# Row-wise argmax over 8192 x 8192 floats: loads and maxima cut into column pieces, index arithmetic gathered into one step

## The chip, the core and the metric

The kernel runs on one core of a Trainium2 chip. The metric is the device time of one execution in microseconds (us). Before the change the median of three runs is 655.53 us (655.39 to 655.56); every run was at a granted clock of 1.0. Times are compared with runs of the kernel before on the same chip, in the same rounds. A ratio is the mean time of one kernel's runs over that of the other's of the same rounds, so it is not quite the ratio of the medians that stand beside it.

Engines in the profile: DVE is VectorE, POOL is GpSimd, ACT is ScalarE, PE is TensorE, SP is SyncE, and SPq is the queue on which SyncE issues loads.

## The reference

```python
def setup_inputs():
    return {"x": np.random.randn(8192, 8192).astype(np.float32)}

def reference(x):
    return np.argmax(x, axis=1)
```

The input has 268 MB and is read once. The output is 8192 integers.

## The kernel before

The rows are worked in 64 tiles of 128 rows; a tile is 128 partitions by 8192 columns, 4 MiB. For each tile, VectorE takes the maximum of each of 128 chunks of 64 columns. For every four tiles a lookup follows: the maximum over the chunks (`mx`), which chunk has it (`match` on GpSimd, then `k` on VectorE), a gather of that chunk from HBM, and the place in it (`match` again, then `k2`). Lookups are put off by some steps, so that VectorE need not wait for GpSimd or the gather. Tiles 62 and 63, the last two, go another way: right after its maxima VectorE finds the largest chunk of such a tile itself (`MAX8` and `FIND_INDEX8` in the timelines), so the second `MAX8` of a timeline marks the end of the last maximum.

```python
xpool = ctx.enter_context(tc.tile_pool(name="x_sbuf", bufs=5))
...
def load_reduce(t, cm, widths):
    xt = xpool.tile([P, M], F32, tag="xt")
    at = 0
    for w in widths:
        keep(nc.sync.dma_start(out=xt[:, at:at + w], in_=x[t * P:(t + 1) * P, at:at + w]))
        at += w
    at = 0
    for w in widths:
        c0, c1 = at // L, (at + w) // L
        keep(nc.vector.reduce_max(
            out=cm[:, c0:c1], in_=xt[:, at:at + w].rearrange("p (c l) -> p c l", l=L), axis=AX.X))
        at += w
        step[0] = t * 4 + at // 2048
        run_due()
...
def finish():                       # the end of a group's lookup
    k2 = spool.tile([P, g], F32, tag="k2")
    keep(nc.vector.reduce_max(out=k2, in_=wl, axis=AX.X))
    r = res[:, t0:t0 + g]
    keep(nc.vector.scalar_tensor_tensor(out=r, in0=k, scalar=float(L), in1=k2, op0=ALU.mult, op1=ALU.add))
    keep(nc.vector.tensor_scalar(out=r, in0=r, scalar1=-1.0, scalar2=float(C * L + L), op0=ALU.mult, op1=ALU.add))
    if t0 + g == 60:
        store(0, 60)
...
for g in [4] * 15 + [2]:
    ...
        load_reduce(t, cm[:, i, :], [M] if t < 60 else [2048] * 4)
    ...
load_reduce(62, cm62, [2048] * 4)
d62 = direct_begin(62, cm62)
load_reduce(63, cm63, [2048] * 3 + [1024, 512, 512])
d63 = direct_begin(63, cm63)
```

Tiles 60 to 63 are already loaded in quarters and smaller pieces; the others come whole, one DMA each.

Of the kernel before, what the change touches and what calls it, by code (L numbers as in the profile page):

```python
# [7 lines left out]
F32 = mybir.dt.float32  # L8
U32 = mybir.dt.uint32
I32 = mybir.dt.int32  # L10
ALU = mybir.AluOpType
AX = mybir.AxisListType
# [3 lines left out]
def kernel(  # L16
# [5 lines left out]
    nc = tc.nc  # L22
    keep = tc.keep_in_program_order
    N, M = x.shape
    P = 128
    C = 128
    L = M // C
    NT = N // P

    xpool = ctx.enter_context(tc.tile_pool(name="x_sbuf", bufs=5))  # L30
    spool = ctx.enter_context(tc.tile_pool(name="small", bufs=3))
    cpool = ctx.enter_context(tc.tile_pool(name="const", bufs=1))
# [30 lines left out]
    keep(nc.gpsimd.tensor_scalar(out=ident, in0=ident, scalar1=0.0, scalar2=None, op0=ALU.is_equal))  # L63

    res = cpool.tile([P, NT], F32)
    o_last = cpool.tile([P, 2], I32)
    nc.gpsimd.memset(o_last, 0)

# [4 lines left out]
    def defer(steps, fn):  # L73
        pending.append((step[0] + steps, fn))
        pending.sort(key=lambda e: e[0])

    def run_due():
        while pending and pending[0][0] <= step[0]:
            pending.pop(0)[1]()

    def load_reduce(t, cm, widths):

        assert sum(widths) == M
# [14 lines that stand above are left out]
    def match(w, vals, mx, desc, g):  # L98

        for i in range(g):  # L100
            keep(nc.gpsimd.tensor_scalar(out=w[:, i, :], in0=vals[:, i, :], scalar1=mx[:, i:i + 1],  # L101
                                         scalar2=None, op0=ALU.is_equal))
            keep(nc.gpsimd.tensor_tensor(out=w[:, i, :], in0=w[:, i, :], in1=desc, op=ALU.mult))  # L103

    def store(t0, n):
        ps = ppool.tile([n, P], F32, tag="ps")
        nc.tensor.transpose(ps, res[:, t0:t0 + n], ident)  # L107
        o = cpool.tile([n, P, 2], I32, tag=f"o{t0}")
        nc.gpsimd.memset(o, 0)  # L109
        keep(nc.scalar.copy(out=o[:, :, 0:1], in_=ps.unsqueeze(2)))  # L110
        keep(nc.scalar.dma_start(out=out_rows[t0:t0 + n, :], in_=o.rearrange("t p two -> t (p two)")))

    def lookup(t0, g, cm, gather_after, match_after):

        mx = spool.tile([P, g], F32, tag="mx")
        keep(nc.vector.reduce_max(out=mx, in_=cm, axis=AX.X))  # L116
        wc = spool.tile([P, g, C], F32, tag="wc")
        match(wc, cm, mx, descC, g)
        k = spool.tile([P, g], F32, tag="k")

        def gather():
            keep(nc.vector.reduce_max(out=k, in_=wc, axis=AX.X))  # L122
            idx = spool.tile([P, g], U32, tag="idx")
            keep(nc.vector.tensor_tensor(out=idx, in0=baseC[:, t0:t0 + g], in1=k, op=ALU.subtract))  # L124
            ga = spool.tile([P, g, L], F32, tag="ga")
            for i in range(g):
                keep(nc.gpsimd.indirect_dma_start(  # L127
                    out=ga[:, i, :], out_offset=None, in_=x_flat[:, :],
                    in_offset=bass.IndirectOffsetOnAxis(ap=idx[:, i:i + 1], axis=0)))
            wl = spool.tile([P, g, L], F32, tag="wl")  # L130
            match(wl, ga, mx, descL, g)

            def finish():
                k2 = spool.tile([P, g], F32, tag="k2")
                keep(nc.vector.reduce_max(out=k2, in_=wl, axis=AX.X))  # L135

                r = res[:, t0:t0 + g]
                keep(nc.vector.scalar_tensor_tensor(out=r, in0=k, scalar=float(L), in1=k2,  # L138
                                                    op0=ALU.mult, op1=ALU.add))
                keep(nc.vector.tensor_scalar(out=r, in0=r, scalar1=-1.0, scalar2=float(C * L + L),  # L140
                                             op0=ALU.mult, op1=ALU.add))
                if t0 + g == 60:
                    store(0, 60)

            defer(match_after, finish)

        defer(gather_after, gather)

    def direct_begin(t, cm):

        m8 = spool.tile([P, 8], F32, tag="m8")
        keep(nc.vector.max(out=m8, in_=cm))  # L152
        c8 = spool.tile([P, 8], U32, tag="c8")
        keep(nc.vector.max_index(out=c8, in_max=m8, in_values=cm))  # L154
        idx = spool.tile([P, 1], U32, tag="idx1")
        keep(nc.vector.tensor_tensor(out=idx, in0=c8[:, 0:1], in1=base[:, t:t + 1], op=ALU.add))  # L156
        ga = spool.tile([P, L], F32, tag="ga1")
        keep(nc.gpsimd.indirect_dma_start(  # L158
            out=ga, out_offset=None, in_=x_flat[:, :],
            in_offset=bass.IndirectOffsetOnAxis(ap=idx[:, :1], axis=0)))  # L160
        return m8, c8, ga

    def direct_end(m8, c8, ga, dst):
        l8 = spool.tile([P, 8], U32, tag="l8")
        keep(nc.vector.max_index(out=l8, in_max=m8, in_values=ga))  # L165
        keep(nc.vector.scalar_tensor_tensor(out=dst, in0=c8[:, 0:1], scalar=float(L), in1=l8[:, 0:1],
                                            op0=ALU.mult, op1=ALU.add))

    t = 0
    for g in [4] * 15 + [2]:  # L170
        cm = spool.tile([P, g, C], F32, tag="cm")
        t0 = t
        for i in range(g):
            load_reduce(t, cm[:, i, :], [M] if t < 60 else [2048] * 4)
            t += 1
        if g == 4:
            lookup(t0, g, cm, 4, 7)
        else:
            lookup(t0, g, cm, 1, 100)

    cm62 = spool.tile([P, C], F32, tag="cm1")
    load_reduce(62, cm62, [2048] * 4)
    d62 = direct_begin(62, cm62)
    cm63 = spool.tile([P, C], F32, tag="cm1")
    load_reduce(63, cm63, [2048] * 3 + [1024, 512, 512])
    d63 = direct_begin(63, cm63)
    step[0] = 1000
    run_due()
    direct_end(*d62, res[:, 62:63])
    store(60, 3)  # L190
    direct_end(*d63, o_last[:, 0:1])
# [31 lines left out]
```

## Time and profile before

| | before |
|---|---|
| time, median | 655.53 us |
| span of the profiled run | 653.8 us |
| VectorE busy | 592.0 us (91%) |
| share of the 16 DMA engines taken by the loads of x | 96.3% |
| a whole tile: spacing of landings, without gathers | 9.71 us |
| a whole tile: its maximum on VectorE | 8.69 us |
| last piece of x lands | 636.7 us |
| VectorE ends the last maximum | 645.2 us |

The prediction below shows the lines that these come from. The chain of work that ended last, by engine (share of the span):

```profile
DMA 77%; DVE 19%; issue 2%; POOL 1%; SPq 0%; POOLq 0%; DVEq 0%
```

### The profile page before, as it was taken

What the parts mean: (1) busy time and instruction counts of PE and PEld (TensorE: products, weight loads), DVE (VectorE), ACT (ScalarE), POOL (GpSimd) and SP (SyncE); (2) the same over time, 40 slices, a digit from 0 to 9 for tenths busy, and PEclk for the clock granted to TensorE, in tenths of its full rate; (3) what the DMA queues carried; (4) which work ended last, traced back from release to release, by engine and by line L of the source; (5) the groups of instructions that cost most, each with busy time, mean ns of one, the idle gap of its engine ahead of it and who ended that gap; (6) DMA issues with size and microseconds to landing.
All of it is one profiled execution on the core that took longest, in us unless ns stands there. A gap on an engine that the chain in (4) does not pass through costs nothing.

```text
span 653.8 us, 739 instructions
## 1 busy us (share of the span) xinstructions
PE 0.8 (0%) x2; PEld 0.2 (0%) x2; DVE 592.0 (91%) x188; ACT 1.8 (0%) x3; POOL 176.0 (27%) x325
## 2 busy tenths in 40 slices
PE   0000000000000000000000000000000000000000
PEld 0000000000000000000000000000000000000000
DVE  2899898998989989998998989989998998989986
ACT  0000000000000000000000000000000000000000
POOL 1004223041241313323041240412323142230550
DMA  9999999999999999999999999999999999999980
GB/s 385 419 447 419 425 447 424 419 433 429 429 425 431 429 429 423 423 443 425 421 439 423 426 425 435 433 424 429 423 437 425 421 443 421 427 425 415 418 341 4
DMA packets 13511, 270.66 MB, mean 414 GB/s; under 512 B 2434, under 2 KB 2497, under 8 KB 3905
## 3 DMA queue, kind: packets, MB, share of 16 engines
q1 hardware_dynamic: 11376, 268.44, 96.3%
q0 software_dynamic: 2048, 2.10, 0.9%
q10 hardware_dynamic: 81, 0.06, 0.0%
q14 instruction: 6, 0.05, 0.0%
HBM read 270.53 MB, written 0.07 MB: 414 GB/s over the span
## 4 chain that ended last, share of the span: by engine, by line
DMA 77%; DVE 19%; issue 2%; POOL 1%; SPq 0%; POOLq 0%; DVEq 0%
DMA xt<-in_x_dram 76%; DVE cm L92 18%; DMA ga<-in_x_dram,idx 1%; POOL ga L127 0%; SPq L87 0%; POOL wc L101 0%; POOL ga L158 0%; DVE k L122 0%; POOL wc L103 0%; DVE mx L116 0%; POOL wl L101 0%; DVE k L135 0%; DVE c L154 0%; DVE idx L124 0%; POOL wl L103 0%
## 5 line engine op out<-in xcount | busy, mean ns | idle before, releaser
L92 DVE TENSOR_REDUCE cm<-xt 128x128 f32<-128x8192 f32 (+2 forms) x78 | 556.9, 7152 | 51.5 <-DMA xt<-in_x_dram 51.5
L101 POOL TENSOR_SCALAR wc<-cm,mx 128x128 f32<-128x128 f32 x62 | 37.2, 601 | 256.3 <-DVE mx L116 256.3
L127 POOL DMA_INDIRECT ga<-in_x_dram,idx x62 | 60.3, 972 | 96.9 <-DVE idx L124 82.9
L101 POOL TENSOR_SCALAR wl<-ga,mx 128x64 f32<-128x64 f32 x62 | 27.6, 445 | 98.2 <-DMA ga<-in_x_dram,idx 98.2
L103 POOL TENSOR_TENSOR wc<-wc,descC 128x128 f32<-128x128 f32 x62 | 28.1, 453 | 5.2
L103 POOL TENSOR_TENSOR wl<-wl,descL 128x64 f32<-128x64 f32 x62 | 19.7, 319 | 5.2
L122 DVE TENSOR_REDUCE k<-wc 128x4 f32<-128x512 f32 (+1 forms) x16 | 10.6, 660 | 1.7 <-POOL wc L103 1.7
L116 DVE TENSOR_REDUCE mx<-cm 128x4 f32<-128x512 f32 (+1 forms) x16 | 10.7, 669 | 0.6
L135 DVE TENSOR_REDUCE k<-wl 128x4 f32<-128x256 f32 (+1 forms) x16 | 6.4, 400 | 0.0
L158 POOL DMA_INDIRECT ga<-in_x_dram,idx x2 | 2.0, 994 | 9.1 <-DVE k L135 8.8
L140 DVE TENSOR_SCALAR res<-res 128x4 f32<-128x4 f32 (+1 forms) x16 | 2.7, 170 | 0.6
L138 DVE SCALAR_TENSOR_TENSOR res<-k,k 128x4 f32<-128x4 f32 (+1 forms) x16 | 2.7, 167 | 0.6
L124 DVE TENSOR_TENSOR idx<-baseC,k 128x4 uint32<-128x4 f32 (+1 forms) x16 | 2.6, 162 | 0.6
L110 ACT CAST o<-ps 60x128 int32<-60x128 f32 (+1 forms) x2 | 0.5, 263 | 645.4 <-PE ps L107 645.4
L165 DVE MATCH_VALUE_LOAD l<-m,ga 128x8 f32 x2 | 0.2, 88 | 1.6 <-DMA ga<-in_x_dram,idx 1.6
L107 PE MATMUL ps<-ident,res 128*60 128x128 f32 (+1 forms) x2 | 0.8, 382 | 646.9 <-DVE res L140 633.3
L110 ACT ACT_TABLE_LOAD x1 | 1.3, 1283 | 0.7 <-PEq L207 0.7
L152 DVE MAX8 m<-cm 128x8 f32<-128x128 f32 x2 | 0.6, 295 | 0.1
L109 POOL MEMSET o<- 60x256 int32 (+1 forms) x2 | 0.6, 302 | 0.0
L154 DVE FIND_INDEX8 c<-m,cm 128x8 uint32<-128x128 f32 x2 | 0.6, 284 | 0.0
L63 POOL TENSOR_SCALAR ident<-ident 128x128 f32<-128x128 f32 x1 | 0.5, 539 | 0.0
L156 DVE TENSOR_TENSOR idx<-c,base 128x1 uint32<-128x1 uint32 x2 | 0.4, 206 | 0.1
(15 smaller groups left out, 2.6 us busy)
## 6 DMA issues: line engine op xcount, KB each, us to landing
xt<-in_x_dram SPq DMA_DIRECT2D x60, 4096.0 KB, 40.6
xt<-in_x_dram SPq DMA_DIRECT2D x15, 1024.0 KB, 21.3
ga<-in_x_dram,idx POOLq DMA_INDIRECT x64, 8.3
xt<-in_x_dram SPq DMA_DIRECT2D x1, 512.0 KB, 17.9
xt<-in_x_dram SPq DMA_DIRECT2D x2, 256.0 KB, 13.8
out_dram<-o ACTq DMA_DIRECT2D x1, 60.0 KB, 2.9
out_dram<-o ACTq DMA_DIRECT2D x1, 3.0 KB
out_dram<-o_last SPq DMA_DIRECT2D x1, 1.0 KB, 3.1
```

Source lines behind the costliest of these rows:

```text
L92: keep(nc.vector.reduce_max(out=cm[:, c0:c1], in_=xt[:, at:at + w].rearrange("p (c l) -> p c l", l=L), axis=AX.X))
L101: keep(nc.gpsimd.tensor_scalar(out=w[:, i, :], in0=vals[:, i, :], scalar1=mx[:, i:i + 1], scalar2=None, op0=ALU.is_equal))
L103: keep(nc.gpsimd.tensor_tensor(out=w[:, i, :], in0=w[:, i, :], in1=desc, op=ALU.mult))
L110: keep(nc.scalar.copy(out=o[:, :, 0:1], in_=ps.unsqueeze(2)))
L116: keep(nc.vector.reduce_max(out=mx, in_=cm, axis=AX.X))
L122: keep(nc.vector.reduce_max(out=k, in_=wc, axis=AX.X))
L124: keep(nc.vector.tensor_tensor(out=idx, in0=baseC[:, t0:t0 + g], in1=k, op=ALU.subtract))
L127: keep(nc.gpsimd.indirect_dma_start(out=ga[:, i, :], out_offset=None, in_=x_flat[:, :], in_offset=bass.IndirectOffsetOnAxis(ap=idx[:, i:i ...
L135: keep(nc.vector.reduce_max(out=k2, in_=wl, axis=AX.X))
L138: keep(nc.vector.scalar_tensor_tensor(out=r, in0=k, scalar=float(L), in1=k2, op0=ALU.mult, op1=ALU.add))
L140: keep(nc.vector.tensor_scalar(out=r, in0=r, scalar1=-1.0, scalar2=float(C * L + L), op0=ALU.mult, op1=ALU.add))
L158: keep(nc.gpsimd.indirect_dma_start(out=ga, out_offset=None, in_=x_flat[:, :], in_offset=bass.IndirectOffsetOnAxis(ap=idx[:, :1], axis=0)))
```

## The change

Its intent is to let VectorE begin on a tile before all of it has landed, to release work sooner, and to save VectorE two small operations for each group of four tiles. Tiles 0 to 47 come in halves, 48 to 61 in quarters, 62 and 63 in quarters and smaller pieces. The index of 60 tiles is computed by two operations on 60 columns instead of by two for each group.

```diff
+    k_all = cpool.tile([P, NT], F32)
+    k2_all = cpool.tile([P, NT], F32)
 ...
+    def combine(t0, n):
+        r = res[:, t0:t0 + n]
+        keep(nc.vector.scalar_tensor_tensor(out=r, in0=k_all[:, t0:t0 + n], scalar=float(L),
+                                            in1=k2_all[:, t0:t0 + n], op0=ALU.mult, op1=ALU.add))
+        keep(nc.vector.tensor_scalar(out=r, in0=r, scalar1=-1.0, scalar2=float(C * L + L),
+                                     op0=ALU.mult, op1=ALU.add))
 ...
             def finish():
-                k2 = spool.tile([P, g], F32, tag="k2")
-                keep(nc.vector.reduce_max(out=k2, in_=wl, axis=AX.X))
-                (two operations for r, as in the kernel before)
+                keep(nc.vector.reduce_max(out=k2_all[:, t0:t0 + g], in_=wl, axis=AX.X))
                 if t0 + g == 60:
+                    combine(0, 60)
                     store(0, 60)
 ...
-            load_reduce(t, cm[:, i, :], [M] if t < 60 else [2048] * 4)
+            load_reduce(t, cm[:, i, :], [4096] * 2 if t < 48 else [2048] * 4)
 ...
-    load_reduce(62, cm62, [2048] * 4)
+    load_reduce(62, cm62, [2048] * 3 + [1024] * 2)
 ...
-    load_reduce(63, cm63, [2048] * 3 + [1024, 512, 512])
+    load_reduce(63, cm63, [2048] * 2 + [1024] * 3 + [512] * 2)
 ...
+    combine(60, 2)
```

More of the change, by code (lines that the diff above doesn't have):

```diff
@@ L118, in lookup @@
         match(wc, cm, mx, descC, g)
-        k = spool.tile([P, g], F32, tag="k")
+        k = k_all[:, t0:t0 + g]
         def gather():
@@ L133, in finish @@
             def finish():
-                k2 = spool.tile([P, g], F32, tag="k2")
-                keep(nc.vector.reduce_max(out=k2, in_=wl, axis=AX.X))
-                r = res[:, t0:t0 + g]
-                keep(nc.vector.scalar_tensor_tensor(out=r, in0=k, scalar=float(L), in1=k2,
-                                                    op0=ALU.mult, op1=ALU.add))
-                keep(nc.vector.tensor_scalar(out=r, in0=r, scalar1=-1.0, scalar2=float(C * L + L),
-                                             op0=ALU.mult, op1=ALU.add))
+                keep(nc.vector.reduce_max(out=k2_all[:, t0:t0 + g], in_=wl, axis=AX.X))
                 if t0 + g == 60:
+                    combine(0, 60)
                     store(0, 60)
```

## The prediction

> **What bounds the kernel now.** I read the page first, then the timeline of VectorE at the start and the end, then the SyncE queue's timeline and windows over the last 60 us.
>
> ```profile
> span 653.8 us, 739 instructions
> PE 0.8 (0%) x2; PEld 0.2 (0%) x2; DVE 592.0 (91%) x188; ACT 1.8 (0%) x3; POOL 176.0 (27%) x325
> ...
> DMA  9999999999999999999999999999999999999980
> ...
> q1 hardware_dynamic: 11376, 268.44, 96.3%
> ```
>
> The 16 DMA engines are full from the first slice to the 38th, while VectorE has idle time in every tile. The queue of x alone takes 96.3% of the span. So the load stream sets the pace, and VectorE follows it. The chain of waits agrees: 76% of the span is "DMA xt", 18% is the maximum of line 92. That share of line 92 is no proof that VectorE bounds: the chain runs through it where a buffer is given back, and the queue is four tiles ahead then. VectorE at the start shows the tile time of the stream without any lookup beside it:
>
> ```profile
> 12.91 8.69 DVE L92 TENSOR_REDUCE cm<-xt 128x128 f32<-128x8192 f32 x1 [12.91 <-DMA xt<-in_x_dram]
> 22.61 8.69 DVE L92 TENSOR_REDUCE cm<-xt 128x128 f32<-128x8192 f32 x1 [1.02 <-DMA xt<-in_x_dram]
> ...
> 51.75 8.69 DVE L92 TENSOR_REDUCE cm<-xt 128x128 f32<-128x8192 f32 x1 [0.30 <-DMA xt<-in_x_dram]
> ```
>
> Each starts when its tile has landed: (51.75 - 12.91) / 4 = 9.71 us a tile, against 8.69 us for its maximum. Later a group of four tiles takes 39.45 us (a reduce waiting for its tile starts at 506.58 and the fourth after it at 546.04), so the group's four gathers cost the stream about 0.6 us.
>
> The end is another matter, and the change is aimed at it. Windows over the end (columns: length, busy time and instructions of each engine, clock, DMA share, GB/s) and VectorE's timeline there:
>
> ```profile
> 633.00:636.00 3.00, 0.39 (x1) 0.13 (x1) 2.93 (x5) 0.27 (x1) 1.23 (x4) 1.00 0.64 227
> 636.00:639.00 3.00, 0.00 (x0) 0.00 (x0) 2.96 (x4) 0.00 (x0) 1.35 (x2) 1.00 0.07 17
> 639.00:645.00 6.00, 0.00 (x0) 0.00 (x0) 6.00 (x5) 0.00 (x0) 0.00 (x0) 1.00 0.00 0
> ```
>
> ```profile
> 636.24 8.97 DVE L92 TENSOR_REDUCE cm<-xt 128x32 f32<-128x2048 f32 x6
> 645.25 0.29 DVE L152 MAX8 m<-cm 128x8 f32<-128x128 f32 x1
> ```
>
> The DMA engines fall silent at about 636 us; the last piece, issued at 624.1, lands 12.6 us later, at 636.7. VectorE has all six pieces of the last tile still before it and ends them at 645.2: 8.5 us after the data. The lag comes from tile 59, the last one taken whole: it lands at 595.3, when VectorE can only begin its 8.69 us. The quarters of tiles 60 to 63 then land faster than it can catch up. From 645.2 to the end (8.6 us) are the last lookup, its gather and the store, which the change leaves alone.
>
> **What the Trainium skill says.** "Perfetto Trace Analysis", section DMA Optimizations: splitting may let work start sooner if DMA engines are generally idle, and larger transfers use the bandwidth better. Here they are not idle (digit 9 in 38 slices), so only the last, uncovered wait can gain. "DMA: Bandwidth & Descriptors", section Why small descriptors are slow: each packet bears a fixed overhead besides its bytes; it gives 3 cycles on 256 B and says the combining of descriptors is worth it only up to 256 B. One would call it nothing at 16 KB. The trace shows more at 8 KB. The pieces of tiles 60 on are issued when an earlier piece has landed (the queue's own waits name landings for 69 issues), so their spacing is the spacing of landings:
>
> ```profile
> 595.33 15.23 SPq L87 DMA_DIRECT2D xt<-in_x_dram  x7
> ```
>
> The seventh issue starts 0.33 us (one issue) before the end of this piece, at 610.23: (610.23 - 595.33) / 6 = 2.483 us for 1 MB, before any gather of this stretch. Four make 9.93 us against 9.71 whole. So three more DMAs cost 0.22 us, **0.074 us for each DMA added** (8 more row packets and one completion write on each of 16 engines). The windows agree: 421 GB/s in 598 to 614, 434 in 13 to 51.7. "Vector Engine (DVE) Microarchitecture Reference", section Measured stream behaviour on trn2: 1.0417 ns a column plus about 75 ns an instruction after overlap. The trace: 8686 ns for 8192 columns, 2276 for 2048, 1204 for 1024, 672 for 512, which is 1.043 ns a column plus 139 ns; back to back they overlap by 81 ns (8.97 us for pieces that sum to 9.38), which leaves 58 (so 2.195 us for a quarter behind another, 1.12 for 1024 columns, 0.59 for 512).
>
> **The change part by part.**
> - *Smaller pieces, the stream.* Tiles 0 to 47 have one more DMA each (48), tiles 48 to 59 three more (36), tiles 62 and 63 one each (2): 86 x 0.074 = **6.4 us later at the end of the stream**, all of it on the path. Of this the halves are 3.6 us, taken by a straight line between two measured sizes. The last landing moves from 636.7 to 643.1.
> - *Smaller pieces, VectorE before the end.* A half should take 1.043 x 4096 + 139 = 4.41 us, two of them 8.82. Even with 0.5 us a tile for lookups that stays under the stream's 9.8, so it costs nothing. The same holds for quarters (8.86 against 9.93).
> - *Smaller pieces, the end.* VectorE now works on pieces as they land and has no 8.69 us lag. I count back from 643.1 with 2.48 us for a 2048-column piece, 1.28 for 1024, 0.68 for 512 (the slope 2.41 us per MB plus 0.074): tile 63 has two, three and two of them, tile 62 three and two, so tile 62's first piece lands at 643.1 - 17.7 = 625.4. Is VectorE free then? Tile 59 lands at 595.3 + 6.2 = 601.5; its last quarter 2.28, tile 60 8.86, tile 61 8.86, and between them two row maxima and a gather step (0.6, 0.8, 0.4) make 21.8: it is done at 623.3 and waits. From 625.4 its work has no room left: tile 62 in 3 x 2.195 + 2 x 1.12 + 0.08 = 8.9; column maximum and index 0.53 (627.39 to 627.92 before); the finish of tiles 56 to 59 with the index step 0.71 (632.31 to 633.02); the direct start of tile 62 0.90; tile 63 in 2 x 2.195 + 3 x 1.12 + 2 x 0.59 = 8.9. Sum 19.95, end **645.4**. The data bound would be 643.1 + 0.7 = 643.8, so VectorE binds the end still, by 1.6 us. The 1.66 us wait for GpSimd before that column maximum should go: GpSimd was done at 627.4, VectorE asks at about 627.7.
> - *Index arithmetic in one step.* 14 of 15 groups lose two small operations, 0.71 - 0.41 = 0.30 us each with gaps, 4.2 us of VectorE. All of it lies in idle time (51.5 us waited for tiles), so it is worth nothing. The one step on 60 columns costs some hundredths more and stays in the end.
> - *Start.* VectorE starts at about 8 instead of 12.9 us; it has only to wait sooner. Worth nothing.
>
> Sum: the last maximum ends at 645.4 instead of 645.2. A gain of 6.2 us of lag is spent on 6.4 us of stream. Time 655.5 + 0.2, rounded for the small extra waits between the pieces in the end to **656.0 us**.
>
> **The rivals.**
> - *Extra DMAs are free.* The stream would end at 636.7 again and VectorE 6.4 us sooner: 649.4 us, 0.9% faster. For it: packets of one engine overlap a little (DMA shares of 1.01 in windows), and the skill's overhead is tiny. Against it: six spacings of 2.483 and 421 GB/s. Between the two lies the case that halves are free and quarters are not: 652.2.
> - *The cost a DMA is larger or gathers suffer more.* Around the first gathers of the end the stream seems slower still (windows 595.3 to 636.7: 396 GB/s, with the edge). A cost of 0.1 us a DMA would add 2.2 us: 658.1. Gathers beside smaller packets may as well land sooner (8.3 us median now, 5.7 in the quarters), which helps no path.
> - *VectorE becomes the bound of the end by waits.* If the column maximum of tiles 60 and 61 still waits 1.7 us for GpSimd, the end moves by that: 657.5.
> - *The queue runs dry with small pieces.* Against it: in the quarters of before a piece was issued 20 us ahead of its landing, the smallest 12.6 us ahead, and the stream held.
>
> **Range and chances.** Free halves give 652.2, costlier DMAs or a kept GpSimd wait some 658. I take **652.2 to 658.6** around 656.0. Faster by over 2% means under 642.4, below what even free DMAs give: 0.01. Slower by over 2% means over 668.6, which takes 0.22 us for each of 86 DMAs, three times what is measured: 0.01. Within 2%: 0.98.
>
> **What would show it.** Right: SyncE's last load lands near 643 instead of 636.7; VectorE ends the last maximum within 3 us of that, near 645.4; tile spacing of halves near 9.78 us and of quarters near 9.93; VectorE waits for DMA in almost every tile up to 61; no wait on GpSimd at the column maximum of tiles 60 and 61. Wrong: a last landing still at 637 (then DMAs are free), a spacing of halves of 9.71 (then only quarters cost), or VectorE over 4 us behind the last landing (then the lag has another source than whole tiles).

## The result

The changed kernel takes 656.65 us (median of 4 runs, 656.56 to 656.73) against 655.49 us for the kernel before in the same rounds. The ratio is 1.0018, with a 95% interval of 1.0000 to 1.0035. A repeat on another chip (the run after_again below) gives 1.0014, 1.0001 to 1.0028. So the change costs about 1 us, 0.15%: nothing by the 2% rule, but not a gain. Yet the profile is far from unchanged.

The page of the changed kernel, with its span, busy times, DMA share in 40 slices and the queue of the loads (packets, MB, share of 16 engines):

```profile
span 655.0 us, 883 instructions
...
PE 0.8 (0%) x2; PEld 0.2 (0%) x2; DVE 596.8 (91%) x246; ACT 1.8 (0%) x3; POOL 175.9 (27%) x325
...
DMA  8999999999999999999999999999999999999992
...
q1 hardware_dynamic: 23760, 268.45, 97.6%
```

The loads move the same bytes in 23760 packets instead of 11376. That is (23760 - 11376) / 16 = 774 more on each DMA engine, which is 86 added DMAs of 8 rows and one completion write. By the digits the DMA engines are full into one slice more (a slice is 16.4 us). The chain that ended last has changed character:

```profile
DMA 94%; issue 2%; DVE 2%; POOL 1%; SPq 0%; POOLq 0%; DVEq 0%
```

VectorE has all but left the chain, 19% to 2%, and the time has not fallen. The chain of before ran through VectorE where a buffer was given back, four tiles ahead of need (a load of a whole tile took 40.6 us from issue to landing, some four tile times). That share was not to be had, as the run with the index arithmetic alone will show.

VectorE's timeline at the start gives the spacing of landings of halves (start, length, engine, line, operation, shapes, and the idle time before with what ended it):

```profile
17.96 4.42 DVE L94 TENSOR_REDUCE cm<-xt 128x64 f32<-128x4096 f32 x1 [0.48 <-DMA xt<-in_x_dram]
...
42.43 4.42 DVE L94 TENSOR_REDUCE cm<-xt 128x64 f32<-128x4096 f32 x1 [0.48 <-DMA xt<-in_x_dram]
```

Each waits for its half to land. The second is five halves after the first: (42.43 - 17.96) / 5 = 4.894 us, so 9.79 us a tile instead of 9.71. For the quarters, the issues of SyncE, which wait for landings as they did before:

```profile
600.29 12.75 SPq L89 DMA_DIRECT2D xt<-in_x_dram  x6
```

The sixth starts 0.33 us before the end: (12.75 - 0.33) / 5 = 2.484 us a quarter, 9.94 us a tile.

The end: windows of 3 us (the last two figures are the DMA share and GB/s), the last issue of a load with its time to landing, and VectorE's timeline:

```profile
639.00:642.00 3.00, 0.00 (x0) 0.00 (x0) 3.00 (x2) 0.00 (x0) 0.09 (x1) 1.00 0.81 312
642.00:645.00 3.00, 0.00 (x0) 0.00 (x0) 3.00 (x4) 0.00 (x0) 0.00 (x0) 1.00 0.07 27
645.00:648.00 3.00, 0.00 (x0) 0.00 (x0) 2.86 (x9) 0.00 (x0) 0.09 (x1) 1.00 0.00 0
```

```profile
L89 SPq DMA_DIRECT2D xt<-in_x_dram x1: 328/328/328, 633.3 to 633.3; - x1
...
DMA to landing us min/median/max: 10.6/10.6/10.6
```

```profile
602.77 2.29 DVE L94 TENSOR_REDUCE cm<-xt 128x32 f32<-128x2048 f32 x1 [0.19 <-DMA xt<-in_x_dram]
...
623.13 2.29 DVE L94 TENSOR_REDUCE cm<-xt 128x32 f32<-128x2048 f32 x1 [0.65 <-DMA xt<-in_x_dram]
...
625.79 2.28 DVE L94 TENSOR_REDUCE cm<-xt 128x32 f32<-128x2048 f32 x1
628.78 0.42 DVE L132 TENSOR_REDUCE k_all<-wc 128x2 f32<-128x256 f32 x1 [0.71 <-POOL wc L105]
...
637.68 9.04 DVE L94 TENSOR_REDUCE cm<-xt 128x32 f32<-128x2048 f32 x7
646.76 0.29 DVE L156 MAX8 m<-cm 128x8 f32<-128x128 f32 x1
```

The last piece lands at 633.3 + 10.6 = 643.9 us; VectorE ends the last maximum at about 646.7. So the sum of the change, in the profiled runs, is:

| | before | after | difference |
|---|---|---|---|
| last landing of x | 636.7 | 643.9 | +7.2 |
| from there to the end of the last maximum | 8.5 | 2.8 | -5.7 |
| from there to the end of the span | 8.6 | 8.3 | -0.3 |
| span | 653.8 | 655.0 | +1.2 |

The expected gain was made: VectorE is no longer a tile behind the data. It was spent on a longer stream. (The 0.3 us after the last maximum lie in the last store and the end of the program, which the change leaves alone.)

### The profile page after: what moved, and what is told of

The parts are those of the page before. It is cut to its first block, busy times and chain, and to the rows that moved or that the text cites. A ratio compares the mean times of both kernels' runs of the same rounds, so it can differ in the third digit from the quotient of the medians.

```text
span 655.0 us, 883 instructions
## 1 busy us (share of the span) xinstructions
PE 0.8 (0%) x2; PEld 0.2 (0%) x2; DVE 596.8 (91%) x246; ACT 1.8 (0%) x3; POOL 175.9 (27%) x325
## 3 DMA queue, kind: packets, MB, share of 16 engines
q1 hardware_dynamic: 23760, 268.45, 97.6%
## 4 chain that ended last, share of the span: by engine, by line
DMA 94%; issue 2%; DVE 2%; POOL 1%; SPq 0%; POOLq 0%; DVEq 0%
DMA xt<-in_x_dram 93%; DMA ga<-in_x_dram,idx 1%; DVE cm L94 1%; POOL ga L137 0%; SPq L89 0%; POOL wc L103 0%; DVE k_all L132 0%; POOL ga L162 0%; POOL wc L105 0%; POOL wl L103 0%; DVE c L158 0%; DVE k_all L144 0%; DVE idx L134 0%; POOL wl L105 0%; DVE l L169 0%
## 5 line engine op out<-in xcount | busy, mean ns | idle before, releaser
L94 DVE TENSOR_REDUCE cm<-xt 128x64 f32<-128x4096 f32 (+3 forms) x164 | 568.9, 3480 | 50.1 <-DMA xt<-in_x_dram 48.9
L132 DVE TENSOR_REDUCE k_all<-wc 128x4 f32<-128x512 f32 (+1 forms) x16 | 10.6, 660 | 0.7 <-POOL wc L105 0.7
L144 DVE TENSOR_REDUCE k_all<-wl 128x4 f32<-128x256 f32 (+1 forms) x16 | 6.4, 401 | 0.0
L134 DVE TENSOR_TENSOR idx<-baseC,k_all 128x4 uint32<-128x4 f32 (+1 forms) x16 | 2.6, 162 | 0.6
## 6 DMA issues: line engine op xcount, KB each, us to landing
xt<-in_x_dram SPq DMA_DIRECT2D x2, 256.0 KB, 10.9
```

The lines of the kernel that those rows point to most:

```text
L94: keep(nc.vector.reduce_max(out=cm[:, c0:c1], in_=xt[:, at:at + w].rearrange("p (c l) -> p c l", l=L), axis=AX.X))
L132: keep(nc.vector.reduce_max(out=k, in_=wc, axis=AX.X))
L134: keep(nc.vector.tensor_tensor(out=idx, in0=baseC[:, t0:t0 + g], in1=k, op=ALU.subtract))
L144: keep(nc.vector.reduce_max(out=k2_all[:, t0:t0 + g], in_=wl, axis=AX.X))
```

## The experiments

The theory: the end gains what VectorE's lag of one whole tile was worth, and each added load delays the full stream by some 0.075 us, wherever it stands. The rivals: added loads are free and something else eats the gain; VectorE's instructions are what bounds the kernel; the halves are free and only the quarters cost.

| run | this, median us | before, same rounds | ratio (95%) |
|---|---|---|---|
| loads_halved | 660.88 | 655.72 | 1.0079 (1.0066 to 1.0093) |
| two_runs_one_load | 660.71 | 655.72 | 1.0078 (1.0064 to 1.0091) |
| maxima_halved | 656.46 | 655.72 | 1.0011 (0.9998 to 1.0025) |
| index_once | 655.74 | 655.72 | 0.9998 (0.9985 to 1.0012) |
| bulk_whole | 652.58 | 655.76 | 0.9953 (0.9939 to 0.9966) |
| all_quarters | 665.70 | 655.76 | 1.0151 (1.0137 to 1.0165) |
| graded | 651.99 | 655.76 | 0.9940 (0.9927 to 0.9954) |
| graded_late_finish | 649.84 | 655.76 | 0.9906 (0.9891 to 0.9922) |
| after_again | 656.62 | 655.80 | 1.0014 (1.0001 to 1.0028) |
| graded_ask_later | 650.37 | 655.80 | 0.9919 (0.9906 to 0.9933) |
| graded_finish_only | 650.94 | 655.80 | 0.9928 (0.9915 to 0.9942) |

All eleven runs gave the right result. Each interval is about 0.9 us wide to either side, so smaller differences below rest on the timelines, not on the times.

### The loads in halves, nothing else

```diff
 (on the kernel before)
-        for w in widths:
+        for w in ([4096] * 2 if t < 60 else widths):
             keep(nc.sync.dma_start(out=xt[:, at:at + w], in_=x[t * P:(t + 1) * P, at:at + w]))
```

> The kernel before with only the loads of tiles 0 to 59 cut into two DMAs; the maximum still takes the whole tile, the end is unchanged. Theory (each DMA added costs the full stream about 0.074 us, and the end keeps its lag of one whole tile): 60 more DMAs make 4.4 us, so 659.9 us, with tiles 9.78 us apart instead of 9.71 where no gather runs. Rival (added DMAs are hidden, and the changed kernel gained nothing for another reason): 655.5 us, within 0.5.

Measured: 660.88 us, 5.2 us more than before, 0.086 us for each of the 60 added loads. VectorE's timeline of this run, first and fourth tile:

```profile
13.04 8.69 DVE L92 TENSOR_REDUCE cm<-xt 128x128 f32<-128x8192 f32 x1 [13.04 <-DMA xt<-in_x_dram]
...
42.40 8.69 DVE L92 TENSOR_REDUCE cm<-xt 128x128 f32<-128x8192 f32 x1 [1.09 <-DMA xt<-in_x_dram]
```

(42.40 - 13.04) / 3 = 9.79 us a tile, as forecast. The rival "added loads are free" falls, and "only quarters cost" with it. The cost is 0.8 us above the expected 4.4; the last load of this run was issued at 629.0 and landed 12.7 us later, at 641.7, which is 5.0 us after that of the kernel before. So most of the excess lies in the stream too, over and above the spacing without gathers.

### Twice the packets in the same number of loads

```diff
 (on the kernel before, tiles 0 to 59; shortened: the rest of the function is as before)
-        xt = xpool.tile([P, M], F32, tag="xt")
-        one load and one maximum of [P, M]
+        xt = xpool.tile([P, 2, M // 2 + 8], F32, tag="xt")
+        keep(nc.sync.dma_start(out=xt[:, :, 0:M // 2],
+                               in_=x[t * P:(t + 1) * P, :].rearrange("p (h m) -> p h m", h=2)))
+        keep(nc.vector.reduce_max(out=cm.rearrange("p (h c) -> p h c", h=2),
+             in_=xt[:, :, 0:M // 2].rearrange("p h (c l) -> p h c l", l=L), axis=AX.X))
```

> The kernel before with each of tiles 0 to 59 loaded by one DMA into a buffer with a gap of 32 bytes in the middle of each row, so that each row takes two runs of 16 KB: twice the packets, the same number of DMAs and completions. This tells what the 0.074 us a DMA consist of. If the packets cost it: 60 x (0.074 less one completion write of 9 ns) = 3.9 us more, 659.4 us. If the DMA with its completion costs it: 655.5 us. If the load then takes many small packets, it says nothing.

Measured: 660.71 us, within 0.2 us of the run before, and 1.3 us above the 659.4 expected for packets alone. From this run's page, the queue and the issues (number, KB each, us to landing), and VectorE's timeline at the first and fourth tile:

```profile
q1 hardware_dynamic: 19056, 268.44, 96.5%
...
xt<-in_x_dram SPq DMA_DIRECT2D x60, 4096.0 KB, 40.8
```

```profile
13.46 8.69 DVE L89 TENSOR_REDUCE cm<-xt 128x128 f32<-128x8192 f32 x1 [13.46 <-DMA xt<-in_x_dram]
...
42.85 8.69 DVE L89 TENSOR_REDUCE cm<-xt 128x128 f32<-128x8192 f32 x1 [1.12 <-DMA xt<-in_x_dram]
```

There are 60 loads of 4 MiB, as before, but 19056 packets: 19056 - 11376 = 7680 = 60 x 128. The cost is that of two loads a tile. So it is the number of row packets that the stream pays for; what the issue, the load's completion and its semaphore cost is less than these rounds can tell (0.9 us in 60 loads). Per engine these are 480 packets more for 5.0 us, about 10 ns each. The spacing agrees: (42.85 - 13.46) / 3 = 9.80 us a tile, 0.09 us for 8 packets, so 11 ns; the prediction's 0.074 us for 8 rows and one completion would be 8 ns. The expectation took 9 ns off for a completion, an estimate that supposes it costs as much as a row; nothing here shows such a saving. A tile is still read as one load in this run, so it is not the gaps between the rows of a half that cost the time. The second half of each row lies 32 bytes further on in the buffer; no run tests that alone.

### The maxima in halves, nothing else

```diff
 (on the kernel before)
-        for w in widths:
+        for w in ([4096] * 2 if t < 60 else widths):
             c0, c1 = at // L, (at + w) // L
             keep(nc.vector.reduce_max(...))
```

> The kernel before with only the maximum of tiles 0 to 59 cut into two instructions; each tile is still one DMA. Theory (VectorE has room in every tile, and only its work after the last whole tile counts): 60 more instructions of 58 to 139 ns lie in idle time, so 655.5 to 655.8 us. Rival (VectorE's instruction count bounds the kernel): 60 x 0.06 to 0.14 makes 659 to 664 us.

Measured: 656.46 us, ratio 1.0011 with an interval that holds 1. It lies 0.7 us above the expected range, which the interval can't tell from nothing, though all five times lie above the nine of the kernel before (656.26 up, 656.07 at most). The rival (3.5 us or more) is outside the interval. The profiled run says where the excess is: tile 47 starts at 477.11 us against 476.98, tile 51 at 517.30 against 516.45, tile 59 at 596.28 against 595.34, and each of them waited for its data. So most of it came in the stream, in one group of four tiles, and not as sixty small costs of VectorE; what slowed that group stays open. Sixty more VectorE instructions in the bulk do not bound the kernel.

### The index arithmetic alone

```diff
 (on the kernel before: k_all, k2_all and combine as in the change; all widths as before)
```

> The kernel before with only the index arithmetic of 60 tiles done in one step. Theory (the 4 us of VectorE saved lie in its idle time; the one step on 60 columns is about 0.1 us longer and lies in the end): 655.5 us, from 655.3 to 655.8. Rival (VectorE's time counts everywhere): up to 4 us less, 651.5 us.

Measured: 655.74 us against 655.72. The page shows what was saved:

```profile
PE 0.8 (0%) x2; PEld 0.2 (0%) x2; DVE 587.3 (90%) x160; ACT 1.8 (0%) x3; POOL 175.9 (27%) x325
```

VectorE is busy for 587.3 us instead of 592.0, with 28 fewer instructions, and the time is the same. This is the plainest case of a saving in idle time.

### The bulk whole, the end as in the change

```diff
 (on the changed kernel)
-            load_reduce(t, cm[:, i, :], [4096] * 2 if t < 48 else [2048] * 4)
+            load_reduce(t, cm[:, i, :], [M] if t < 48 else [2048] * 4)
```

> The changed kernel with tiles 0 to 47 whole again; quarters from tile 48 on and everything else as in the change. Theory (the halves of the bulk only slow the stream, by 0.074 to 0.085 us a tile, and twelve tiles of quarters are enough for VectorE to catch up): 3.6 to 4.1 us less than the changed kernel's 656.6, so 652.5 to 653.1 us, last landing near 640. Rival (the halves cost nothing, only quarters do): 656.6 us. Rival (VectorE can't catch up from a whole tile in twelve quarters): last landing near 640 but VectorE 5 us or more behind it, 655 us or more.

Measured: 652.58 us, faster than both kernels. The last load was issued at 629.2 and landed after 10.6 us, at 639.8, which is 4.1 us sooner than in the changed kernel; VectorE ended at 642.2, 2.4 us behind it. So twelve tiles of quarters are enough to catch up from a whole tile, and the halves of the bulk cost about 4 us for nothing (4.1 us of stream for 48 loads, 0.085 each).

### Everything in quarters

```diff
 (on the changed kernel)
-            load_reduce(t, cm[:, i, :], [4096] * 2 if t < 48 else [2048] * 4)
+            load_reduce(t, cm[:, i, :], [2048] * 4)
```

> The changed kernel with tiles 0 to 47 in quarters, not halves. Theory (a constant cost for each added set of row packets): 96 DMAs more at 0.074 to 0.085 us make 7.1 to 8.2 us, so 663.7 to 664.8 us, tiles 9.93 us apart without gathers. If the cost grew with smaller packets or vanished between halves and quarters, the step would be clearly off this.

Measured: 665.70 us, 0.9 us above the range. The last load was issued at 640.8 and landed at 651.4, which is 7.5 us after the changed kernel's for 96 added loads: 0.078 us each, as expected. Tiles without gathers came 9.95 us apart (expected 9.93). VectorE ended 7.5 us later as well (654.26 against 646.76). The rest, 9.4 us from there to the end of the span instead of 8.2, is in the last lookup and store; in this profile the last store alone took 4.1 us from issue to landing against 3.0 in the changed kernel. Why it was slower is not settled. The cost of a load is about the same for halves (0.085 us above) and quarters (0.078).

### Graded sizes

```diff
 (on the changed kernel)
-            load_reduce(t, cm[:, i, :], [4096] * 2 if t < 48 else [2048] * 4)
+            load_reduce(t, cm[:, i, :], [M] if t < 52 else [4096] * 2 if t < 60 else [2048] * 4)
```

> The changed kernel with tiles 0 to 51 whole, 52 to 59 in halves, 60 to 63 as in the change: 10 DMAs more than the kernel before, not 86. Theory: the stream ends 76 x 0.074 = 5.6 us sooner than the changed kernel's (last landing near 638.2). VectorE catches up from the whole tile during the eight tiles of halves (8 x 0.6 us against 4.3) and starts the quarters about half a tile behind, of which some 0.5 us should be left at the end: 651 to 652 us, so faster than both kernels by about 0.6%. Rival (the end needs twelve tiles of quarters): VectorE stays 6 us or more behind the last landing, 654 us or more.

Measured: 651.99 us, at the upper edge of the range. The last load landed at 627.2 + 10.9 = 638.1, as expected. VectorE's timeline of this run:

```profile
623.76 0.42 DVE L132 TENSOR_REDUCE k_all<-wc 128x2 f32<-128x256 f32 x1 [1.40 <-POOL wc L105]
...
632.67 9.04 DVE L94 TENSOR_REDUCE cm<-xt 128x32 f32<-128x2048 f32 x7
641.74 0.29 DVE L156 MAX8 m<-cm 128x8 f32<-128x128 f32 x1
```

VectorE ends 3.6 us behind the data, after a wait of 1.4 us for GpSimd. Ten added loads, not 86, buy most of the gain of the end (4.9 us of lag instead of 5.7). Against the run with the whole bulk the stream ends 1.7 us sooner, but VectorE is 1.2 us further behind, so the 0.6 us between these two times are not told apart by the intervals.

### Taking work and the wait out of the end

```diff
 (on the graded kernel; both edits: graded_late_finish)
-            lookup(t0, g, cm, 4, 7)
+            lookup(t0, g, cm, 4, 7 if t0 < 56 else 100)    # finish of tiles 56 to 59 behind the last maximum
-            lookup(t0, g, cm, 1, 100)
+            lookup(t0, g, cm, 2, 100)                      # ask one piece later
-                if t0 + g == 60:
-                    combine(0, 60)
-                    store(0, 60)
+                if t0 + g == 56:
+                    combine(0, 56)
+                    store(0, 56)
-    combine(60, 2)
+    combine(56, 6)
-    store(60, 3)
+    store(56, 7)
```

> The same sizes as the graded run; besides, the finish of tiles 56 to 59 with the index step moves behind the last maximum, where VectorE waits 1.7 us for the last gather anyway (the store of the first 56 tiles goes out early, of the last 7 at the end), and the column maximum of tiles 60 and 61 is asked one piece later, so that GpSimd is done (0.7 us waited in the changed kernel). Theory (VectorE binds the end by about 2 us, so what leaves its end counts in full): 0.8 and up to 0.7 us less than the graded run, 649.5 to 651 us. Rival (the data bound the end): the same as the graded run within 0.3.

> The graded run with one of the two late edits alone: the column maximum of tiles 60 and 61 is asked one piece later. Theory: VectorE's wait of 1.4 us for GpSimd in the graded run goes, and as VectorE binds the end, the time falls by about 1.2 us from the graded run's 652.0, to 650.6 to 651.0 us. Rival (the edit only moves the wait, or GpSimd's later gather delays the end): 651.8 us or more.

> The graded run with the other late edit alone: the finish of tiles 56 to 59 with the index step behind the last maximum. Theory: 0.8 us of VectorE leave the end, where it is always busy, and lie in the 1.7 us it waits for the last gather: 651.1 to 651.4 us. Rival (the moved work delays the last lookup or the last store): 652 us or more. Together the two edits gave 2.1 us less than the graded run, so the two should about add up to that.

Measured: 650.37 us with the later ask alone, 650.94 with the late finish alone, 649.84 with both. Against the kernel before of their own rounds, the graded run saves 3.8 us, the later ask 5.4, the late finish 4.9, both 5.9. Each alone is worth what it takes from VectorE's end or a little more (1.7 and 1.1 us against 1.4 and 0.8). These two came 0.2 us below their expected ranges. Both together are worth 2.1 us, in the expected range but less than their sum, which was expected to add up. These tenths are within the intervals, so VectorE's timelines must decide: the second `MAX8` starts at 641.74 in the graded run, 640.19 with the later ask, 640.88 with the late finish and 639.86 with both, so 1.9 us for both against 1.6 and 0.9. The run with both:

```profile
630.75 9.08 DVE L94 TENSOR_REDUCE cm<-xt 128x32 f32<-128x2048 f32 x7
639.86 0.29 DVE L156 MAX8 m<-cm 128x8 f32<-128x128 f32 x1
```

The last load of this run lands at 626.4 + 11.9 = 638.3 us, and the last piece of 512 columns takes 0.67 us. VectorE ends at 639.8, 0.9 us above what that piece allows. But an earlier piece holds it already: the second piece of tile 63 is issued at 613.9 and lands 19.0 us later, at 632.9, and VectorE starts on it at 632.97, where the later ask alone had it start at 633.33. Of the 0.8 us that the late finish takes away only 0.4 could come off there; more work taken out before this piece would only make VectorE wait. Neither late edit was tried on the kernel before. This version is the fastest, 0.9% below the kernel before and 1.0% below the changed one.

### The changed kernel again

> The changed kernel once more, unaltered, beside the kernel before on another chip and in five rounds, to narrow the interval of its ratio (1.0000 to 1.0035). Theory: 1.0015 to 1.002, about 1 us slower, since the stream's loss and the end's gain nearly cancel. If it were noise: a ratio whose interval lies around 1.000.

Measured: 656.62 against 655.80 us, ratio 1.0014 (1.0001 to 1.0028). The small loss is real as far as two chips can say, though both intervals only just leave out 1.

## Why the prediction was right

The time (656.65 us) lies in the range and 0.65 us from the value. That it is so near is in part luck: the working gave 655.7, to which 0.3 was added for small waits that it did not count; the last maximum ended 1.3 us later than foretold, and the stretch after it was 0.3 us shorter, which no step foretold. By its steps:

- **The stream bounds, VectorE follows.** Right. The index run took 4.7 us of busy time off VectorE at no gain; the maxima run added 60 instructions at no clear loss; 60 loads alone cost 5.2 us.
- **0.074 us for each added load, halves on a straight line.** Right in kind, a little small: 9.79 us a tile for halves and 9.94 for quarters, where 9.78 and 9.93 were foretold, but the last landing came 7.2 us later where 6.4 was foretold. The 0.074 was read from six spacings. A longer stretch gives more; these are the last pieces of tiles 3 and 47 in the kernel before, the changed kernel and the run with everything in quarters, each waiting for its data:

```profile
42.04 8.69 DVE L92 TENSOR_REDUCE cm<-xt 128x128 f32<-128x8192 f32 x1 [1.03 <-DMA xt<-in_x_dram]
476.98 8.69 DVE L92 TENSOR_REDUCE cm<-xt 128x128 f32<-128x8192 f32 x1 [0.46 <-DMA xt<-in_x_dram]
```

```profile
480.91 4.42 DVE L94 TENSOR_REDUCE cm<-xt 128x64 f32<-128x4096 f32 x1 [0.47 <-DMA xt<-in_x_dram]
```

```profile
42.77 2.29 DVE L94 TENSOR_REDUCE cm<-xt 128x32 f32<-128x2048 f32 x1 [0.21 <-DMA xt<-in_x_dram]
488.32 2.29 DVE L94 TENSOR_REDUCE cm<-xt 128x32 f32<-128x2048 f32 x1 [0.21 <-DMA xt<-in_x_dram]
```

Over 44 tiles with their gathers this is 9.885 us a tile before, (480.91 - 42.43) / 44 = 9.966 in halves and 10.126 in quarters: 0.080 us for each added load both times, and 86 x 0.080 = 6.9 us. (The repeat of the changed kernel gives 0.085, so the last figure is not firm.) One might suspect that gathers cost more beside smaller packets. The traces do not bear it out: over the same tiles the halved loads cost 0.088 us a tile, more than without gathers (0.077), but the two runs in one load, with packets of the same size, 0.072, less than without (0.086). The remaining 0.3 us is not explained. Tiles 48 to 59 alone came 3.5 us later for their 36 added loads, 0.097 each (602.77 - 480.91 against 595.34 - 476.98), and the last four tiles made up some of it; why is open.

- **The lag of a whole tile goes.** Right. VectorE waits for the last quarter of tile 61 (0.65 us at 623.13), so it has caught up.
- **VectorE still binds the end, by 1.6 us.** Right in kind; it was 2.8 - 0.7 = 2.1 us. The late edits, made on the graded kernel, agree: what was taken from VectorE's end came off the time until the data held it. One slip: the working has VectorE done with tile 61 at 623.3 and idle until 625.4, but by its own count the last quarter of tile 61 lands only at 625.4 - 2.48 = 622.9 and takes 2.28 us. So there is no idle time, and tile 62 begins only behind the maxima of tile 61 and the `mx` of tiles 60 and 61, at 625.79.
- **The 1.66 us wait for GpSimd should go.** This step failed: the wait shrank to 0.71 us and stayed on the path. It took GpSimd's end from the kernel before, 627.4. But GpSimd does these two tiles after the gathers of tiles 56 to 59, and those can only be issued when tile 60 is done, which the slower stream delays: the first gather started at 616.07 instead of 614.59. GpSimd was done at 628.7, and VectorE, which asked at 628.07, waited for it (the line at 628.78 above). A time that hangs on the stream was used as if it were fixed. The first gather and VectorE's wait in the kernel before, then the first gather in the changed one:

```profile
614.59 1.05 POOL L127 DMA_INDIRECT ga<-in_x_dram,idx  x1 [5.26 <-DVE idx L124]
...
627.39 0.42 DVE L122 TENSOR_REDUCE k<-wc 128x2 f32<-128x256 f32 x1 [1.66 <-POOL wc L103]
```

```profile
616.07 1.05 POOL L137 DMA_INDIRECT ga<-in_x_dram,idx  x1 [5.71 <-DVE idx L134]
```

Starting tile 62 at 625.8 instead of 625.4 and this wait make 1.1 of the 1.3 us by which VectorE ended later than foretold (646.7 and not 645.4).

- **Index arithmetic: nothing.** Right, shown by its own run.
- **Extra loads are free, halves are free.** Both rivals fell with the halved loads and the whole bulk.

## What to carry to other kernels

With the DMA engines full, as here, splitting the loads did not bring the last data sooner; it added packets to a full stream, and only the work behind the last byte could be shortened. So split at the end alone, no earlier than the consumer needs to catch up, and with sizes that step down: here 10 added loads did what 86 had been spent on. Then look at what the consumer does in that end besides the data, and move it into a wait that is there anyway.

## What the Trainium skill lacked or had wrong

- "DMA: Bandwidth & Descriptors", section Why small descriptors are slow, speaks of packets of 256 B and finds combining worth it only up to there. In these runs the packet count still shows at 16 KB a row: 9.79 us for 4 MiB against 9.71 at 32 KB, 9.94 at 8 KB. That is 8 to 11 ns for each packet on each engine. The same page gives 10.5 ns a packet in a note to its measured table, but as the whole time of a packet where 64 of them carry 4 KB, issued from GpSimd; that the numbers are alike may be chance.
- The same page's Rules for kernel authors give 1 MiB or more per DMA for the highest bandwidth. The size of the DMA was not what counted: 4 MiB loads cut into two runs a row were as slow as 2 MiB loads (660.71 and 660.88 us). The number of contiguous row pieces counted.
- "Perfetto Trace Analysis", section DMA Optimizations, ties splitting to idle DMA engines. It lacks the case that they are full but the consumer lags at the end: 10 split loads gave 0.6% and, with two late edits, 0.9%.
- "Vector Engine (DVE) Microarchitecture Reference", section Measured stream behaviour on trn2, has about 75 ns an instruction after overlap; the maxima here showed 58 ns (139 ns less 81 ns of overlap), nearer to the 60 ns of "Perfetto Trace Analysis", section Optimizing Scalar/DVE Operations. The slope of 1.043 ns a column agrees with its 1.0417.
